# A decoder block on one core: the cross attention's query projection as seven products of halves, its norm factor in the exponential

## The chip, the core and the metric

The kernel runs on one core of a Trainium2 chip. The core has five engines that run beside each other and meet through semaphores: TensorE (PE in the profile, its weight loads PEld), VectorE (DVE), ScalarE (ACT), GpSimd (POOL) and SyncE (SP), which here only starts transfers between the chip's main memory and the core's own SBUF. TensorE writes its sums into PSUM, from which VectorE and ScalarE read them. Each engine works through its own list of instructions in order. The metric is the device time of one execution in microseconds (us).

## The reference, cut to what matters

All is float32, one batch, 512 positions (rows), width 1024, memory of 256 rows. The change lies in the second of three parts of the block:

```
x = x + mixed @ w_out                        # end of the first part
hc    = rms_norm(x, g_cross)                 # x * rsqrt(mean(x*x)+eps) * g, row by row
mem_n = rms_norm(mem, g_mem)
q = (hc @ w_cq)                              # 512x1024 @ 1024x1024, 4 heads of 256
k, v = split(mem_n @ w_ckv)
s = einsum('bshd,bmhd->bhsm', q, k) * 256 ** -0.5
p = softmax(s, axis=-1)
x = x + einsum('bhsm,bmhd->bshd', p, v) @ w_co
hm = rms_norm(x, g_mlp)
x = x + square(relu(hm @ w_up)) @ w_down     # 1024 -> 4096 -> 1024
return rms_norm(x, g_final)
```

## The kernel before

Every float32 factor is split into two halves of lower precision, `hi` and `lo` (`split`: ScalarE rounds the value to `hi`, VectorE subtracts it to get `lo`), and each product is three matmuls, hi by hi, hi by lo and lo by hi, into the same PSUM tile (`mm3`, lines 105 to 107). Activations lie transposed: 128 of the 1024 features on the partitions, positions along the free axis, so a full tile is 128 x 512 and a projection of width 1024 has eight of them. One such tile takes 8 x 3 = 24 matmuls of 512 columns.

**Weights.** All weight blocks, 128 x 1024 each, stand in one list in the order of use. `weights(i)` loads up to four blocks ahead through SP (`wraw`, 3 buffers) and splits up to three ahead (`whi`, `wlo`, 3 buffers each, lines 111 and 112).

**Order.** TensorE runs the program in the order in which it is written. Work of another kind is put between the matmuls by `after(steps, fn)`: a counter goes up by one with every `tick()` (one `mm3` in a projection), and `fn` is emitted when the count is reached; `flush()` emits all that is due. The order on VectorE, ScalarE and the queues is set by a scheduler at build time, from dependences and priorities. Tiles come from pools by tag with a fixed number of buffers; an allocation waits until the oldest tile of its tag has been read for the last time. PSUM has `acc` (2 buffers), `sc` (3), `tr` (2) and `av`.

**The stages around the change, in order:**

- `projection("out", ...)` makes the output projection of the first part, tile by tile. Behind each tile m, `done_out` calls `residual` (line 576: VectorE adds the tile to x, giving `vr`), then `scaled` (ScalarE makes `hi` of x times the gain, VectorE `lo`, line 267) into a pair of tag `xg`, and `accumulate` (ScalarE squares, VectorE adds into `ss`, line 263). `settle()` runs between the first three tiles' parts; it loads x again and puts `mem_in`, the scaling of the memory, into the queue.
- `mem_k(m)`, eight tiles of 128 x 256 in PSUM `acc`, 24 matmuls of 256 columns each. VectorE multiplies each by the memory's norm factor (line 628) and the result is split into `mix`. `stats1`, 16 ticks behind the output projection, sums `ss` over the partitions with two matmuls against ones (lines 236 and 237, behind a split of `ss`) and makes the norm factor `r1` as a full 128 x 512 tile (`rstd_full`). `mem_v`, 96 matmuls of 512 columns, follows.
- The query projection `cq`: eight tiles of 24 matmuls of 512 columns, the first in `sc`, the others in `acc`. VectorE takes each out of PSUM times `r1`/16 (line 734), then it is split into a pair of tag `s`.
- `cross_scores(h)` for head h: 24 matmuls of 256 columns into two `sc` tiles; maximum (line 688), exponential with row sums (line 692), reciprocal and scaling. `cross_transpose(h)`: 8 transposes on TensorE (line 707) into two `tr` tiles, split into an `at` tile. `cross_out(h)`: two `acc` tiles of 6 matmuls of 512 columns each, weights from `mix` (the memory's values), right side from `at`; each tile is split into `xg`. Heads 0, 1 and 2 have their scores, and 0 and 1 their transposes, between the matmuls of `cq`. Behind it stand `cross_out(0)`, scores 3, transposes 2, `cross_out(1)`, `cross_out(2)`; transposes 3 and `cross_out(3)` come 2 and 7 ticks into the next projection.
- `projection("co", ...)`, then `done_co`: residual, and `right_factors(m, t)`, which makes for the MLP's up projection the seven right factors named B11, T1, T2, T3, T4, B21, B22 from halves of the feature axis and of the positions. `up_set` then makes each 512 x 512 block of the up projection from seven products instead of eight (`block_product`, 24 matmuls of 256 columns, twice per product); four left factors are sums of weight quarters (s1 to s4), s1 and s3 made by a second load that GpSimd's queue adds on (`accum_op`), s2 and s4 by VectorE (`combined`).
- `renew()`, between parts of `co`, closes the pool `early` and opens `late` in its space.

Of the kernel before, what the change touches and what calls it, by code (L numbers as in the profile page):

```python
# [50 lines left out]
def block_kernel(ctx: ExitStack, tc: tile.TileContext, x0g, xT, memT, wv, wm, wst, wdn, wckv, wpool, vecs, csts, idn, gfin, out):  # L51
# [5 lines left out]
    late = {}  # L57
# [17 lines left out]

    def sb(tag, shape, bufs, dt=F32):
        p = apool if tag in EARLY_TAGS else late["pool"] if tag in LATE_TAGS else pool
        return p.tile(shape, dt, tag=tag, name=nm(tag), bufs=bufs)
# [73 lines left out]
    def part(n, name):  # L152
        return wst[4 * n + PARTS.index(name)]

    def load(i):
        if i >= len(blocks):
            return
        if isinstance(blocks[i], tuple):
            n, name = blocks[i]
            if name in ("s1", "s3"):  # L160
                first, then = ("A22", "A21") if name == "s1" else ("A21", "A11")
                if (n, name) not in raw:
                    r = fetch((n, name), part(n, first), "mraw", 5)
                    nc.gpsimd.dma_start(r, part(n, then), accum_op=ALU.add)  # L164
            elif name in PARTS:
                fetch((n, name), part(n, name), "mraw" if name == "A11" else "wraw", 5 if name == "A11" else 3)
# [8 lines left out]
    def combined(n, name):  # L175

        if name in ("s2", "s4"):
            r = raw[n, "s1"]
            V.tensor_tensor(r, r, raw[n, "A11" if name == "s2" else "A12"], op=ALU.add)
            return r  # L180
        return raw[n, name]

    def prep(i):
# [3 lines left out]
        r = combined(*blocks[i]) if isinstance(blocks[i], tuple) else raw[i]  # L187
        if i in SPARE:
            hi, lo = (sb("mix", [P, 2, T], 8, F32R).rearrange("p a t -> p (a t)") for _ in range(2))
        elif i >= FIRST_UP and i % 5 > 2:  # L190
# [16 lines left out]
    def weights(i):  # L207
        far = 4 if i >= FIRST_UP else 0
        for j in range(i, i + 4 + far):
            if j < FIRST_UP or late:  # L210
                load(j)
        for j in range(i, i + 3 + far // 2):
            if j < FIRST_UP or late:
# [87 lines left out]
    WU, WQ, WK, WGATE, WOUT, WCQ, WCO = 0, 4, 8, 12, 20, 28, 36  # L301
# [15 lines left out]
    for m in range(KC):  # L317
        where["cq", m] = add(wm[WCQ + m])
# [3 lines left out]
    for g in range(NG):  # L322
        for n in (2 * g, 2 * g + 1):
            for name in FIRST_ORDER if n == 0 else ORDER:
                where[n, name] = add((n, name))
# [248 lines left out]
    def residual(m, o, g=None, ss=None, nxt=None, tag=None):  # L574
        t = res[m]
        V.tensor_tensor(t, o, t, op=ALU.add)
        if ss is None:
            return
        pr = pair(tag, 8)
        scaled(pr[:, 0, :], pr[:, 1, :], t, vec[:, g + m:g + m + 1])  # L580
        accumulate(ss, m, t)
        nxt[m] = (pr[:, 0, :], pr[:, 1, :])
# [69 lines left out]

    ss1 = sb("ss", [P, T], 1)
    x1g = {}

    def done_out(m, o):
        residual(m, o, G_CROSS, ss1, x1g, "xg")

    def settle():
        flush()  # L660
        for m in range(KC):
# [7 lines left out]
    def stats1():  # L669
        st["r1"] = rstd_full(sp1, ss1)  # L670
# [6 lines left out]
    def cross_scores(h):  # L677
        es = []
        for j in range(NT // 2):
            o = ps("sc", 3)  # L680
# [49 lines left out]
    for m in range(KC):  # L730
# [4 lines left out]
        pr = pair("s", 6)  # L735
        split(pr[:, 0, :], pr[:, 1, :], t)
        st["cq", m] = (pr[:, 0, :], pr[:, 1, :])
        if m in (1, 3, 5):
            after(5, cross_scores, m // 2)
        if m in (3, 5):  # L740
            after(2, cross_transpose, m // 2 - 1)
# [10 lines left out]
    right = {n: {} for n in ("B11", "T1", "B21", "B22", "T2", "T3", "T4")}  # L752
    xs, half, rest = {}, {}, []
    A, B = slice(0, M), slice(M, T)

    def parts(name, k, hi, lo, c):
        right[name][k] = (hi[:, c], lo[:, c])

    def right_factors(m, t):

        k = m % 4
        g = vec[:, G_MLP + m:G_MLP + m + 1]
        x = tmp()
        pr = pair("mix", 8)
        if m < 4:
            b12 = tmp()[:, :M]
            S.activation(x[:, A], t[:, A], AF.Copy, scale=g)
            S.activation(b12, t[:, B], AF.Copy, scale=g)
            V.tensor_tensor(x[:, B], x[:, A], b12, op=ALU.subtract)
            xs[k] = (x[:, B], b12)  # L770
            split(pr[:, 0, :], pr[:, 1, :], x)
            parts("B11", k, pr[:, 0, :], pr[:, 1, :], A)
            parts("T1", k, pr[:, 0, :], pr[:, 1, :], B)
            return
        S.activation(x, t, AF.Copy, scale=g)
        t1, b12 = xs[k]
        y = tmp()
# [270 lines left out]
```

## Time and profile before

| | |
|---|---|
| median of 3 runs | 720.37 us (720.23 to 720.95) |
| profiled execution | 720.76 us |
| its span | 719.0 us |
| mean granted clock of TensorE | 0.996 |
| busy: PE, PEld | 707.0 us (98%), 614.4 us |
| busy: DVE, ACT, POOL | 484.7, 409.2, 66.9 us |

The profile shows one execution. The span runs from the first to the last record; the execution's own time is 1.76 us longer. A row of the timeline gives start, duration, engine, source line, operation, output tile <- input tiles and the shape; in brackets stands how long the engine stood idle before it and what ended that. Matmuls overlap in a pipeline, so a matmul's own duration (0.39 us) is longer than the step from one start to the next, and a pace is read from the starts. Numbers behind tile names are left out of the trace.

### The profile page before, as it was taken

Reading aid. Unit: us, or ns where it says so; the run is one execution under the profiler, and the core shown is the slowest. Engines: PE = TensorE matmul, PEld = TensorE weight load, DVE = VectorE, ACT = ScalarE, POOL = GpSimd, SP = SyncE. Lnnn points to the kernel's source line nnn. Section 1 sums busy time; section 2 is a strip of 40 time slices with the busy share of each in tenths; the row PEclk is TensorE's granted clock in tenths of the full one; section 3 lists DMA queues with packets and bytes.
Section 4 is the critical chain, followed back from the end, with each engine's and each line's share of the span. In section 5 each row is a group of like instructions: output and inputs, shape, how many; then the busy total and the mean of one; then the engine's idle time right before and its main releaser. Section 6 shows DMA issues by size and latency. Waiting matters only on the chain.

```text
span 719.0 us, 10284 instructions
## 1 busy us (share of the span) xinstructions
PE 707.0 (98%) x3958; PEld 614.4 (85%) x3958; DVE 484.7 (67%) x761; ACT 409.2 (57%) x691; POOL 66.9 (9%) x59
## 2 busy tenths in 40 slices
PE   9999999999999999999999999999999999999995
PEld 6887887788889888888889988899889998899884
DVE  7597999976888645573886953688337864478633
ACT  7498998677766434352668742377215752257522
POOL 0044111545000000000100000000000000000000
PEclk9999999999999999999999999999999999999998
DMA  8433223143525552213934642268215672043211
GB/s 317 150 118 117 87 76 117 60 131 134 176 89 175 177 167 70 86 58 114 268 88 119 211 141 88 57 180 250 105 54 176 147 234 88 30 118 118 89 59 58
DMA packets 27521, 91.62 MB, mean 127 GB/s; under 512 B 3120, under 2 KB 3248, under 8 KB 27472
## 3 DMA queue, kind: packets, MB, share of 16 engines
q1 hardware_dynamic: 24976, 82.18, 33.7%
q0 software_dynamic: 2352, 8.52, 6.8%
q8 instruction: 31, 0.51, 0.3%
q10 hardware_dynamic: 144, 0.26, 0.1%
q14 instruction: 18, 0.15, 0.1%
HBM read 86.76 MB, written 2.10 MB: 124 GB/s over the span
## 4 chain that ended last, share of the span: by engine, by line
PE 89%; ACT 5%; DVE 4%; issue 1%; POOL 0%; DVEq 0%; ACTq 0%
PE acc L105 14%; PE acc L107 13%; PE acc L106 13%; PE sc L105 10%; PE sc L107 10%; PE sc L106 10%; PE tr L105 4%; PE tr L107 4%; PE tr L106 4%; PE sc L389 1%; ACT tmp L451 1%; PE sc L391 1%; PE sc L393 1%; ACT whi L111 1%; DVE tmp L449 1%
## 5 line engine op out<-in xcount | busy, mean ns | idle before, releaser
L111 ACT CAST whi<-wraw 128x1024 fp32r<-128x1024 f32 (+1 forms) x92 | 95.2, 1035 | 126.5 <-PE tr L107 50.6
L112 DVE TENSOR_TENSOR wlo<-wraw,whi 128x1024 fp32r<-128x1024 f32 (+1 forms) x92 | 112.9, 1228 | 46.4 <-ACT whi L111 45.7
L105 PE MATMUL acc<-xg,whi 128*128 128x512 f32 x256 | 102.1, 399 | 0.0
L107 PE MATMUL acc<-xg,wlo 128*128 128x512 f32 x256 | 100.0, 391 | 0.0
L106 PE MATMUL acc<-xg,whi 128*128 128x512 f32 x256 | 99.7, 390 | 0.0
L107 PEld LDWEIGHTS acc<-xg,wlo 128*128 128x128 f32 x256 | 48.0, 188 | 10.5
L105 PEld LDWEIGHTS acc<-xg,whi 128*128 128x128 f32 x256 | 48.1, 188 | 9.2
L106 PEld LDWEIGHTS acc<-xg,whi 128*128 128x128 f32 x256 | 48.2, 188 | 9.0
L105 PE MATMUL sc<-mix,whi 128*128 128x256 f32 (+1 forms) x184 | 54.9, 298 | 0.0
L164 POOL DMA_DIRECT2D mraw<-wst x16 | 13.9, 866 | 436.7 <-DMA mraw<-wst 357.9
L107 PE MATMUL sc<-mix,wlo 128*128 128x256 f32 (+1 forms) x184 | 54.1, 294 | 0.0
L106 PE MATMUL sc<-mix,whi 128*128 128x256 f32 (+1 forms) x184 | 54.0, 293 | 0.0
L840 DVE SCALAR_TENSOR_TENSOR vr<-acc,sums,vr 128x512 f32<-128x512 f32 x16 | 12.0, 751 | 49.5 <-PE acc L107 49.5
L894 DVE TENSOR_TENSOR tmp<-sc,tmp 128x512 f32<-128x512 f32 x56 | 37.8, 686 | 9.0 <-PE sc L107 8.6
L111 ACT CAST mhl<-wraw 128x1024 fp32r<-128x1024 f32 x18 | 18.9, 1051 | 38.2 <-PE tr L106 27.4
L111 ACT CAST whi<-mraw 128x1024 fp32r<-128x1024 f32 x24 | 25.0, 1050 | 23.3 <-PE tr L107 8.9
L112 DVE TENSOR_TENSOR wlo<-mraw,whi 128x1024 fp32r<-128x1024 f32 x24 | 29.1, 1221 | 10.1 <-ACT whi L111 10.1
L107 PEld LDWEIGHTS sc<-mix,wlo 128*128 128x128 f32 x184 | 34.6, 188 | 1.1
L105 PEld LDWEIGHTS sc<-mix,whi 128*128 128x128 f32 x184 | 34.6, 188 | 1.0
L106 PEld LDWEIGHTS sc<-mix,whi 128*128 128x128 f32 x184 | 34.5, 187 | 1.1
L105 PE MATMUL sc<-s,whi 128*128 128x256 f32 x112 | 31.4, 281 | 0.0
L106 PE MATMUL sc<-s,whi 128*128 128x256 f32 x112 | 31.2, 279 | 0.0
(300 smaller groups left out, 1974.5 us busy)
## 6 DMA issues: line engine op xcount, KB each, us to landing
wraw<-wm SPq DMA_DIRECT2D x44, 512.0 KB, 3.3
wraw<-wdn SPq DMA_DIRECT2D x32, 512.0 KB, 5.1
mraw<-wst SPq DMA_DIRECT2D x24, 512.0 KB, 4.4
wraw<-wckv SPq DMA_DIRECT2D x16, 512.0 KB, 3.2
mraw<-wst POOLq DMA_DIRECT2D x16, 512.0 KB, 7.2
wraw<-wst SPq DMA_DIRECT2D x16, 512.0 KB, 3.4
s<-s SPq DMA_DIRECT2D x8, 256.0 KB, 3.7
vr<-xT SPq DMA_DIRECT2D x8, 256.0 KB, 5.3
```

The source lines that it names most:

```text
L105: nc.tensor.matmul(o, lh, rh, start=start, stop=False)
L106: nc.tensor.matmul(o, lh, rl, start=False, stop=False)
L107: nc.tensor.matmul(o, ll, rh, start=False, stop=stop)
L111: S.copy(hi, src)
L112: eng.tensor_tensor(lo, src, f(hi), op=ALU.subtract)
L164: nc.gpsimd.dma_start(r, part(n, then), accum_op=ALU.add)
L389: nc.tensor.matmul(o[i], xg[k][0][:, tb], wh[:, c], start=k == 0, stop=False)
L391: nc.tensor.matmul(o[i], xg[k][1][:, tb], wh[:, c], start=False, stop=False)
L393: nc.tensor.matmul(o[i], xg[k][0][:, tb], wl[:, c], start=False, stop=k == KC - 1)
L449: V.tensor_tensor_reduce(e[:, :n], o[:, :n], mask[:, T - n:], -0.125, 3.0e38, ALU.add, ALU.min, mn)
L840: V.scalar_tensor_tensor(y, o, sums[:, 2 * NT + t:2 * NT + t + 1], y, op0=ALU.mult, op1=ALU.add)
L894: V.tensor_tensor(u[new], o, u[old], op=ALU.add)
```

## The change

**The query projection.** `cq` becomes two sets, n = 0 and 1, of four of the eight tiles each. A set is made from seven products of halves (`seven`, cut out of `up_set` with the same order and the same sums): each `block_product` is 2 x 4 `mm3` of 256 columns. The seven results are combined on VectorE by seven additions (`plus`) into four quarters C11, C12, C21, C22, and each is split into `s` pairs (`quads`). The right factors are made in `done_out` by the class `Right` (made out of `right_factors`; the MLP uses it too): `add(m)` for m < 4 makes B11 and T1; for m >= 4 it makes B21, B22, T2, T3, and through `finish` T4. These now go to `xg` and `mfac` pairs. The weights of `cq` come as quarters (`wcq`): s1 and s3 by an added second load on GpSimd's queue, s2 and s4 by an addition on VectorE, as for the up projection.

**The norm's factor.** `stats1` makes it per position on the partitions (`rstd_rows`) instead of as a full tile. The scores are made from the unnormed query; in `cross_scores` the factor (/16) multiplies the maximum (a new 128 x 1 VectorE multiplication) and is the `scale` of the exponential.

**Pools and order.** `early` is closed in `settle()`, a new pool `mid` with tags `mfac` (6) and `mraw` (3) stands in its place until `renew()`. Transposed probabilities go to `mfac` pairs. Scores 1 and 0 now go to `acc` tiles, 2 and 7 ticks into the second set, transposes 1 and 0 at ticks 23 and 26. Behind it stand scores 3, `cross_out(1)`, scores 2, `cross_out(0)`, transposes 3, `cross_out(3)`; transposes 2 and `cross_out(2)` come 2 and 7 ticks into `co`. `co` takes its last inputs in another order.

```diff
+    class Right(dict):
...
+        def add(self, m):
+
+            k, t, g = m % 4, res[m], self.gain(m)
+            x = tmp()
+            pr = pair(*self.pair)
+            if m < 4:
+                S.activation(x, t, AF.Copy, scale=g)
+                V.tensor_tensor(x[:, B], x[:, A], x[:, B], op=ALU.subtract)
+                self.kept[k] = x[:, B]
+                split(pr[:, 0, :], pr[:, 1, :], x)
...
+                return
+            S.activation(x, t, AF.Copy, scale=g)
+            b12 = tmp()[:, :M]
+            S.activation(b12, res[k][:, B], AF.Copy, scale=self.gain(k))
+            y = tmp()
+            V.scalar_tensor_tensor(y[:, A], x[:, B], -1.0, self.kept[k], op0=ALU.mult, op1=ALU.subtract)
+            V.tensor_tensor(y[:, B], x[:, B], b12, op=ALU.subtract)
+            p2 = pair(*self.pair2)
+            split(p2[:, 0, :], p2[:, 1, :], y)
...
+        def finish(self, k, x, y, pr):
+            split(pr[:, 0, :], pr[:, 1, :], x)
+            V.scalar_tensor_tensor(y[:, A], y[:, A], -1.0, x[:, A], op0=ALU.mult, op1=ALU.subtract)
...
+            split(self.half[:, 0, c], self.half[:, 1, c], y[:, A])
...
+    rcross = Right(G_CROSS, "xg", 8, "mfac", 6)
 
     def done_out(m, o):
-        residual(m, o, G_CROSS, ss1, x1g, "xg")
+        residual(m, o)
+        accumulate(ss1, m, res[m])
+        rcross.add(m)
+        if m == KC - 1:
+            rcross.last()
...
     def stats1():
-        st["r1"] = rstd_full(sp1, ss1)
+        r = rstd_rows(sp1, NT)
+        st["r1"] = [r[:, 2 * i:2 * i + 1] for i in range(NT)]
+        V.tensor_scalar(r, r, 1.0 / 16.0, None, op0=ALU.mult)
...
-                c = slice(b * M, (b + 1) * M)
-                S.activation(e[:, c], o[:, c], AF.Exp, bias=mx[:, b:b + 1], accum_out=sm[:, b:b + 1])
+                c, r = slice(b * M, (b + 1) * M), st["r1"][2 * j + b]
+                V.tensor_tensor(mx[:, b:b + 1], mx[:, b:b + 1], r, op=ALU.mult)
+                S.activation(e[:, c], o[:, c], AF.Exp, bias=mx[:, b:b + 1], scale=r, accum_out=sm[:, b:b + 1])
...
-        t = sb("at", [P, NT, T], 2, F32R)
-        pt = (t[:, :MT, :], t[:, MT:, :])
+        pt = pair("mfac", 6), pair("mfac", 6)
...
-    for m in range(KC):
-        o = acc() if m else ps("sc", 3)
-        tile_mm(o, W("cq", m), x1g)
-        t = tmp()
-        V.scalar_tensor_tensor(t, o, 1.0 / 16.0, st["r1"], op0=ALU.mult, op1=ALU.mult)
...
+        seven("cq", n, ORDER, rcross, finish)
+
+    cross_query(0)
+    after(2, cross_scores, 1, "acc", 2)
+    after(7, cross_scores, 0, "acc", 2)
+    after(23, cross_transpose, 1)
+    after(26, cross_transpose, 0)
+    cross_query(1)
     flush()
+    cross_scores(3, "sc", 3)
+    cross_out(1)
+    cross_scores(2, "sc", 3)
     cross_out(0)
-    cross_scores(3)
-    cross_transpose(2)
-    cross_out(1)
-    cross_out(2)
-    after(2, cross_transpose, 3)
-    after(7, cross_out, 3)
+    cross_transpose(3)
+    cross_out(3)
+    after(2, cross_transpose, 2)
+    after(7, cross_out, 2)
```

**Where instructions move.** The first place is VectorE between the residual of the last tile of the output projection (the rows that read `acc_2183` before, `acc_2240` after) and the reading of the first `mem_k` tile out of PSUM (line 628 before, 629 after). Before:

```order
L576 TENSOR_TENSOR vr_1903<-acc_2183,vr_1903 128x512
L112 TENSOR_TENSOR wlo_2229<-wraw_2184,whi_2228 128x1024
L267 SCALAR_TENSOR_TENSOR xg_2215<-vr_1903,vx_67,xg_2215 128x512
L263 TENSOR_TENSOR ss_1822<-ss_1822,tmp_2218 128x512
L112 TENSOR_TENSOR wlo_2265<-wraw_2226,whi_2264 128x1024
L112 TENSOR_TENSOR tmp_2222<-ss_1822,tmp_2221 128x512
L628 TENSOR_TENSOR tmp_2256<-acc_2225,mrstd_2139 128x256
```

After, without the first six of the nineteen rows that begin with `vr_1907<-acc_2240` (they are that residual, three splits of right factors and two steps of the memory's norm):

```order
L116 TENSOR_TENSOR wlo_2299<-wraw_2241,whi_2298 128x1024
L232 SCALAR_TENSOR_TENSOR mrstd_2182<-tmp_2183,mrstd_2182 128x256
L116 TENSOR_TENSOR mfac_2231<-tmp_2228,mfac_2231 128x512
L268 TENSOR_TENSOR ss_1822<-ss_1822,tmp_2272 128x512
...
L116 TENSOR_TENSOR wlo_2335<-wraw_2296,whi_2334 128x1024
L701 SCALAR_TENSOR_TENSOR tmp_2228<-tmp_2228,tmp_2223 128x256
L116 TENSOR_TENSOR xg_2276<-tmp_2275,xg_2276 128x512
L116 TENSOR_TENSOR wlo_2389<-wraw_2332,whi_2388 128x1024
L116 TENSOR_TENSOR tmp_2292<-ss_1822,tmp_2291 128x512
L629 TENSOR_TENSOR tmp_2326<-acc_2295,mrstd_2182 128x256
```

Seven rows from the residual to that reading became nineteen. The sum of squares' split (`tmp_2292<-ss_1822`), on which the next matmuls of `stats1` wait, moved behind them too.

The second place is TensorE at the end of the cross attention: the last transposes there (line 707 before, 776 after) and the `cross_out` of the same head. Before, for head 3, inside the first tile of `co`:

```order
L707 MATMUL tr_3263<-ident_70,tmp_3166 128x128 x4
L707 MATMUL tr_3270<-ident_70,tmp_3188 128x128 x4
L105 MATMUL sc_3255<-xg_3216,whi_3002 128x512
L106 MATMUL sc_3255<-xg_3216,whi_3002 128x512
L107 MATMUL sc_3255<-xg_3216,wlo_3003 128x512
...
L105 MATMUL sc_3295<-xg_3137,whi_3097 128x512
L106 MATMUL sc_3295<-xg_3137,whi_3097 128x512
L107 MATMUL sc_3295<-xg_3137,wlo_3098 128x512
L105 MATMUL acc_3299<-at_3262,mix_2674 128x512
```

After, for head 3, ahead of `co` (`mfac_3506` and `mfac_3507` are the halves of the transposed probabilities):

```order
L776 MATMUL tr_3508<-ident_70,tmp_3386 128x128 x4
L776 MATMUL tr_3515<-ident_70,tmp_3410 128x128 x4
L109 MATMUL acc_3522<-mfac_3506,mix_2753 128x512
L110 MATMUL acc_3522<-mfac_3507,mix_2753 128x512
L111 MATMUL acc_3522<-mfac_3506,mix_2753 128x512
```

Fifteen matmuls of `co` stood between the transposes of head 3 and the first matmul that reads them; now none does. The same stretch of `co` matmuls stands between transposes and `cross_out` of head 2.

More of the change, by code (lines that the diff above doesn't have):

```diff
@@ L74, in block_kernel @@
     LATE_TAGS = ("mraw", "mhl", "sums", "few")
+    MID_TAGS = ("mfac", "mraw")
     def sb(tag, shape, bufs, dt=F32):
+        if tag in MID_TAGS and not late:
+            return mid["pool"].tile(shape, dt, tag=tag, name=nm(tag), bufs=bufs)
         p = apool if tag in EARLY_TAGS else late["pool"] if tag in LATE_TAGS else pool
@@ L150, in fetch, with part @@
         return raw[key]
-    def part(n, name):
-        return wst[4 * n + PARTS.index(name)]
+    def part(key, name):
+        return (wcq if key[0] == "cq" else wst)[4 * key[1] + PARTS.index(name)]
     def load(i):
@@ L316, in block_kernel @@
             where["mv", half, k] = add(wckv[KC + 4 * half + k])
-    for m in range(KC):
-        where["cq", m] = add(wm[WCQ + m])
+    FIRST_CQ = len(blocks)
+    for n in range(2):
+        for name in ORDER:
+            where["cq", n, name] = add(("cq", n, name))
     for m in CO_ORDER:
@@ L729, in block_kernel, with seven, plus @@
     mem_v(1)
-    for m in range(KC):
-        o = acc() if m else ps("sc", 3)
-        tile_mm(o, W("cq", m), x1g)
-        t = tmp()
-        V.scalar_tensor_tensor(t, o, 1.0 / 16.0, st["r1"], op0=ALU.mult, op1=ALU.mult)
[L735 to L741, printed above, removed]
+    def seven(key, n, order, factors, finish):
+        u, five = {}, None
+        def plus(new, o, old):
+            if new not in u:
+                u[new] = tmp()
+            V.tensor_tensor(u[new], o, u[old], op=ALU.add)
+        for name in order:
+            o = ps("sc", 3)
+            block_product(W(key, n, name), factors[RIGHT[name]], o)
+            if name == "A11":
+                u["P1"] = tmp()
+                S.copy(u["P1"], o)
+            elif name == "s2":
+                plus("U2", o, "P1")
+            elif name == "s1":
+                five = o
+            elif name == "s3":
+                plus("U3", o, "U2")
+                plus("C22", five, "U3")
+                u["U4"] = u["U2"]
+                plus("U4", five, "U2")
+                finish("22", u["C22"], -1.0)
+            elif name == "A12":
+                plus("C11", o, "P1")
+                finish("11", u["C11"], 1.0)
+            elif name == "A22":
+                u["C21"] = u["U3"]
+                plus("C21", o, "U3")
+                finish("21", u["C21"], -1.0)
+            elif name == "s4":
+                u["C12"] = u["U4"]
+                plus("C12", o, "U4")
+                finish("12", u["C12"], 1.0)
@@ L753, in block_kernel @@
[L753 to L777, printed above, removed]
-        V.scalar_tensor_tensor(y[:, A], x[:, B], -1.0, t1, op0=ALU.mult, op1=ALU.subtract)
-        V.tensor_tensor(y[:, B], x[:, B], b12, op=ALU.subtract)
-        p2 = pair("s", 6)
-        split(p2[:, 0, :], p2[:, 1, :], y)
-        parts("T2", k, p2[:, 0, :], p2[:, 1, :], A)
-        parts("T3", k, p2[:, 0, :], p2[:, 1, :], B)
-        parts("B21", k, pr[:, 0, :], pr[:, 1, :], A)
-        parts("B22", k, pr[:, 0, :], pr[:, 1, :], B)
-        if m < KC - 1:
-            right_rest(k, x, y, pr)
-        else:
-            rest.append((k, x, y, pr))
@@ L800, in done_co @@
+    right = Right(G_MLP, "mix", 8, "s", 6)
     def done_co(m, o):
@@ L802, in done_co @@
             residual(m, o)
[L803 removed]
+            right.add(m)
         if m == KC - 1:
[L805 to L806 removed]
+            right.last()
     def renew():
         flush()
[L811 removed]
+        middle.close()
         late["pool"] = ctx.enter_context(tc.tile_pool(name="late", bufs=1))
[L814 removed]
+    projection("co", cross_o, [0, 1, 2, 3, 6, 7], [4, 5], done_co, renew, CO_ORDER)
     sums = sb("sums", [P, 24], 1)
@@ L924, in down_part, with finish @@
+    def up_set(n, act, j0):
+        q = quads("xg", 8, act.__setitem__, j0)
+        def finish(c, t, sign):
+            hi, lo = q[c]
+            t = two(t)
+            S.activation(t, t, AF.Relu, scale=sign)
+            S.activation(t, t, AF.Square)
+            split(hi, lo, t)
+        seven("up", n, FIRST_ORDER if n == 0 else ORDER, right, finish)
     def down_part(o, t, act, ks, wt, first, last):
```

180 lines of the change are left out of this document (85 added, 95 removed).

## Prediction

> **What bounds the kernel now.** I read the page first: its engines, then the busy time by stretches of the span, then the timeline of TensorE and VectorE at the places the change touches.
>
> ```profile
> span 719.0 us, 10284 instructions
> PE 707.0 (98%) x3958; PEld 614.4 (85%) x3958; DVE 484.7 (67%) x761; ACT 409.2 (57%) x691; POOL 66.9 (9%) x59
> ```
>
> TensorE is busy for 98% of the span, so it bounds the kernel, and only two things count: what its matmuls take, and every wait that arises in its list. VectorE has a third of its time free on the whole, but that is a mean. The next rows (stretch; its length, then busy time and instructions of PE, PEld, DVE, ACT, POOL; granted clock) are the memory's keys, the whole stretch from the query projection to the next projection, and the end of the kernel.
>
> ```profile
> core 0: us, PE busy (x) PEld busy (x) DVE busy (x) ACT busy (x) POOL busy (x), PEclk, DMA share, GB/s
> 215.00:237.00 22.00, 22.00 (x186) 21.70 (x185) 18.35 (x28) 12.98 (x20) 0.00 (x0) 1.00 0.50 168
> 259.50:326.30 66.80, 66.39 (x349) 56.70 (x348) 40.41 (x70) 28.47 (x62) 0.00 (x0) 1.00 0.24 79
> 711.00:712.00 1.00, 0.23 (x1) 0.00 (x0) 0.73 (x1) 0.00 (x0) 0.00 (x0) 1.00 0.65 250
> 712.00:713.00 1.00, 0.00 (x0) 0.00 (x0) 0.18 (x2) 0.72 (x2) 0.00 (x0) 1.00 0.00 0
> 713.00:714.00 1.00, 0.00 (x0) 0.00 (x0) 0.46 (x3) 0.41 (x2) 0.00 (x0) 0.73 0.00 0
> 714.00:715.00 1.00, 0.00 (x0) 0.00 (x0) 0.92 (x3) 0.72 (x1) 0.00 (x0) 0.50 0.00 0
> ```
>
> In the keys' stage TensorE never waits, though VectorE is already busy for 18.35 of 22 us there: it's close to the next bound exactly where the change adds VectorE work just ahead. In the 66.8 us of the attention it waits 0.41 us in all.
>
> **The matmuls saved.** The paces come from starts 24 or 18 matmuls apart: the first pair is one tile of the query projection, the second 18 matmuls of the keys.
>
> ```profile
> 264.94 0.39 PE L105 MATMUL acc<-xg,whi 128*128 128x512 f32 x1
> 270.38 0.39 PE L105 MATMUL acc<-xg,whi 128*128 128x512 f32 x1
> 234.94 0.28 PE L105 MATMUL acc<-s,whi 128*128 128x256 f32 x1
> 237.06 0.40 PE L105 MATMUL sc<-whi,s 128*128 128x512 f32 x1
> ```
>
> 5.44 us / 24 = 0.2268 us for 512 columns; 2.12 / 18 = 0.1178 us for 256. Before, 8 x 24 = 192 wide ones take 43.5 us. After, 2 sets x 7 products x 24 = 336 narrow ones take 39.6 us. The whole stage, from its first matmul to the first of the next projection, takes 66.9 us:
>
> ```profile
> 259.46 0.40 PE L105 MATMUL sc<-xg,whi 128*128 128x512 f32 x1
> 326.34 0.40 PE L105 MATMUL sc<-xg,whi 128*128 128x512 f32 x1
> ```
>
> The saving is 4.0 us, not the eighth (5.4 us) that the count of products promises: two narrow ones take 0.0088 us more than a wide one. The Trainium skill (TensorE: Matmul & The Clock Gate, Part 2) gives an isolated spacing of N/2.4 + 2.5 ns, 215.8 and 109.2 ns; by it an estimate of the saving is 4.7 us. The trace's spacing is wider at both widths and decides here.
>
> **VectorE ahead of the keys.** This is the largest term. The keys' tiles have two PSUM buffers, so the third tile can't start before VectorE has read the first (line 628). What stands on VectorE from the last output tile to that reading, and when the third tile starts (its first matmul is the last row; above it are three rows of the memory's norm, for the price of narrow ones):
>
> ```profile
> 207.52 0.42 DVE L224 SCALAR_TENSOR_TENSOR tmp<-tmp,ssm 128x256 f32<-128x256 f32 x1
> 207.86 0.15 DVE L224 SCALAR_TENSOR_TENSOR rscr<-rscr,rscr 128x4 f32<-128x4 f32 x1
> 207.97 0.43 DVE L227 SCALAR_TENSOR_TENSOR mrstd<-tmp,mrstd 128x256 f32<-128x256 f32 x1
> ...
> 214.07 0.69 DVE L576 TENSOR_TENSOR vr<-acc,vr 128x512 f32<-128x512 f32 x1 [2.14 <-PE acc L107]
> 214.92 1.23 DVE L112 TENSOR_TENSOR wlo<-wraw,whi 128x1024 fp32r<-128x1024 f32 x1 [0.16 <-ACT whi L111]
> 216.06 0.75 DVE L267 SCALAR_TENSOR_TENSOR xg<-vr,vx,xg 128x512 fp32r<-128x512 f32 x1
> 216.72 0.68 DVE L263 TENSOR_TENSOR ss<-ss,tmp 128x512 f32<-128x512 f32 x1
> 217.86 1.23 DVE L112 TENSOR_TENSOR wlo<-wraw,whi 128x1024 fp32r<-128x1024 f32 x1 [0.45 <-ACT whi L111]
> 219.00 0.69 DVE L112 TENSOR_TENSOR tmp<-ss,tmp 128x512 fp32r<-128x512 f32 x1
> 219.60 0.42 DVE L628 TENSOR_TENSOR tmp<-acc,mrstd 128x256 f32<-128x256 f32 x1
> ```
>
> ```profile
> 219.75 0.48 PE L237 MATMUL tr<-tmp,ones 128*128 128x512 f32 x1
> 220.07 0.38 PE L105 MATMUL acc<-s,whi 128*128 128x256 f32 x1
> ```
>
> From start to start, 1024 columns cost 1.14 us (214.92 to 216.06), 512 cost 0.60 (219.00 to 219.60), 256 cost 0.34 (207.52 to 207.86), a tiny one 0.1. Before, the reading ends at 220.02, and the third tile starts at 220.07: it was just in time, as two keys' tiles and the two matmuls of the norm's sum give 5.65 + 0.47 us of cover. After, nineteen instructions stand from the residual through the reading: three of 1024 (3.42), seven of 512 (4.20), eight of 256 (2.72) and a tiny one (0.1), 10.4 us, with the last one's end (0.42 - 0.34) 10.5. The start, 214.07, stays: between the residuals of the last two output tiles VectorE has one of 1024, four of 512, four of 256 and a tiny one, 5.0 us, in the 5.4 us that a tile takes TensorE. So the reading ends at 224.6 and the third tile starts there, not at 220.07: 4.5 us. VectorE also has to wait for ScalarE's rounding in such a row (0.16 and 0.45 us above); I add 0.2 and take **+4.7 us** (bounds 4.5 and 5.5). Below 4.5 it can't go while these instructions stand in this order: an engine works its list off in order, and VectorE had no free time within the row apart from the bracketed waits. From then on VectorE has 1.14 + 0.34 + 0.34 us per tile of 2.83 us and doesn't fall behind again; the norm's smaller form and its tile-wide steps, dropped later, are covered in the same way.
>
> **The clock after that wait.** TensorE then stands for over 4 us with at most one matmul of the norm's sum in it. At the end of the kernel the last matmul ends at 711.23; the granted clock is 1.00 up to 713, 0.73 in the next microsecond, then 0.50: it halves about 2.2 us after the last matmul. What a restart costs shows only at the start of the run.
>
> ```profile
> 1.19 3.60 PE L127 MATMUL acc<-tmp 128*128 128x512 bf16 x8 [1.19 <-DVE tmp L124]
> 4.90 1.62 PE L389 MATMUL sc<-whi,xg 128*128 128x512 f32 x3
> 6.32 0.63 PE L389 MATMUL av<-whi,xg 128*128 128x512 f32 x1
> 6.75 0.93 PE L391 MATMUL sc<-whi,xg 128*128 128x512 f32 x3
> ```
>
> Eight wide matmuls take 3.60 us, 0.45 each, twice the 0.2268 of later; full pace comes between 6.3 and 6.8, about 5.3 us after the first. Half of that time is lost: 2.7 us at most. At least it costs nothing (the wait is too short after all). I take **+2.2 us**, nearer to the upper row. The Trainium skill (the same page, Part 1) puts the drop after a whole idle window of about 3.4 us and the return after as long a busy one; by it the loss would be 1.7 us (an estimate), and a wait of 4.7 us needn't hold a whole window. The trace's drop 2.2 us after the last matmul is sooner than such a window allows, if its start is counted from there.
>
> **The query stage itself.** VectorE's busy 40.4 us get six more weight splits (14 for 8, 6.8 us), four sums of weights (4.6), 14 additions in place of eight readings (3.6) and 16 tiny multiplications (1.6): 57 us of about 64. It's close, but order and prices let it keep step; I take 0 (bounds 0 and the rival below). The waits at the end move:
>
> ```profile
> 323.43 0.50 PE L105 MATMUL acc<-at,mix 128*128 128x512 f32 x1 [0.41 <-DVE xg L112]
> 327.72 1.03 PE L707 MATMUL tr<-ident,tmp 128*128 128x128 f32 x8
> 328.51 0.47 PE L105 MATMUL sc<-xg,whi 128*128 128x512 f32 x1
> 328.42 1.08 ACT L111 CAST at<-tr 128x512 fp32r<-128x512 f32 x2 [1.29 <-PE tr L707]
> 329.03 1.29 DVE L112 TENSOR_TENSOR at<-tr,at 128x512 fp32r<-128x512 f32 x2 [1.19 <-ACT at L111]
> ```
>
> Before, the split of head 3's transposes ends at 329.03 + 1.29 = 330.32, 1.6 us after they do (327.72 + 1.03); fifteen matmuls of the next projection covered that. After, `cross_out(3)` follows at once and its second matmul needs the lower half: **+1.6 us** (1.3 to 2.2, as the splits of `cross_out(0)`, 0.6 us each, may stand ahead). The 0.41 us wait goes, as scores 2 now stand between: **-0.4**. Transposes 2 keep their fifteen matmuls of cover.
>
> **Later stages.** For m < 4 ScalarE makes one 512-wide scaling in place of two of 256, for m >= 4 one of 256 more; in `co` each tile gives them 5.5 us, so nothing. `up_set` issues the same instructions. 0.
>
> **Sum**, against the profiled execution's own 720.76 us (span 719.0 and 1.76 around it): -4.0 + 4.7 + 2.2 + 1.6 - 0.4 = +4.1, so 724.9. That execution is 0.39 above the median; on the median's scale, **724.5 us**.
>
> **The rivals.**
>
> - *No drop of the clock* (0.22): the wait stays, but the one matmul in it or the few microseconds keep the clock. Then +1.9, 722.3. Speaks for it: only one drop is in the trace, at an end where nothing follows.
> - *The second load of the weights comes late* (0.16). s1 of the second set must be loaded, added to by GpSimd's queue, split, and used before the scores that free the `acc` tiles.
>
> ```profile
> mraw<-wst SPq DMA_DIRECT2D x24, 512.0 KB, 4.4
> mraw<-wst POOLq DMA_DIRECT2D x16, 512.0 KB, 7.2
> ```
>
> The first load can only go when a `mraw` buffer comes free (three here, five for the up projection): VectorE's split of the first set's s3, asked for with the third of the set's products of 24 x 0.1178 = 2.83 us, at 5.7, and done by the prices above at some 8.7 us into the stage. With 4.4 and 7.2 us it lands at 20.3; its split is asked for with the eighth product, at 7 x 2.83 = 19.8. Behind that split on ScalarE and VectorE stands the softmax of head 1, which frees the `acc` tiles for the scores of head 0, due at 27.6. That work takes about 5 us, so from a landing at 22.5 on TensorE waits, microsecond for microsecond. An added load half as long again (3.6 us more) gives +1.4, one twice as long +5: 725.9 to 729.5.
> - *The keys' wait doesn't arise, or is made up* (0.09): VectorE needn't be late if the row of nineteen takes 6.0 us, to 220.07, in place of 10.5. Then -4.0 + 1.6 - 0.4 = -2.8, 717.6, faster. Against it: the prices are measured in the same stage, and nothing later could pay back, since all TensorE waits after it in the attention sum to 0.41 us.
> - *The narrow matmuls save nothing* (0.03): the change keeps its word only if 256 columns cost under 0.13 us in the query too (43.5 / 336). The keys, with the same shapes, show 0.1178. Without the saving it is 728.5.
>
> **How the numbers follow.** The forecast case (0.50) is 724.5, with its bounds (clock +0.5 or, of a drop, -1.0; keys +0.8 or -0.2; `cross_out` +0.6 or -0.3) 723.0 to 726.4. No drop gives 721.8 to 723.7, the late load up to 729.5. The range 721.0 to 728.5 leaves out the faster case and the ends of the late load. A difference under 0.2%, 1.4 us, can't be told from none in this kernel: 718.9 to 721.8 holds a third of the no-drop case, if the saving comes out larger, and part of the faster case, 0.11 in all; faster is 0.08; slower, the rest, 0.81.
>
> **What would show it.** In the profile after: a wait of 4 us or more at the first matmul of the third keys' tile or at the second matmul of the norm's sum, put down to VectorE; a granted clock of 0.5 in a slice soon after, and keys' matmuls 0.24 us apart there; query matmuls 0.1178 apart and from the first of them to the first of `co` 64 us instead of 66.9 (-4.0 + 1.6 - 0.4); a wait of 1.3 to 2.2 us at the second matmul of `cross_out(3)`. It is wrong if the third keys' tile starts within 2 us of the second's end, or if TensorE waits over 1 us anywhere within the two query sets; a clock of 1.00 throughout would strike the 2.2.

## The result and the profile after

The changed kernel takes 731.6 us (median of 4 runs, 730.69 to 732.54), the kernel before 720.3 in the same session: 1.0155 times as long, 95% interval 1.0137 to 1.0173. It is slower, as forecast, but by 11.3 us and not by 4.1, and lies outside the range. The profiled execution took 730.69 us with a span of 728.9, so the trace accounts for 9.9 us against the 719.0 of before.

The page of the changed kernel, engines and the chain that ended last:

```profile
span 728.9 us, 10708 instructions
PE 707.5 (97%) x4108; PEld 621.1 (85%) x4108; DVE 507.4 (70%) x818; ACT 425.0 (58%) x719; POOL 70.4 (10%) x63
...
PE 82%; DVE 8%; ACT 6%; DMA 2%; issue 1%; POOL 0%; SPq 0%; DVEq 0%; ACTq 0%
```

TensorE's busy time has hardly moved, the span has grown, and the chain now runs through transfers (DMA 2%), which it didn't before. The trace is cut at three starts on TensorE. The first key matmul (line 105 before, 109 after) starts at 213.87 before and here, as the next rows show, at 216.50; the first query matmul and the first of `co` follow (before: 259.46 and 326.34):

```profile
216.50 0.28 PE L109 MATMUL acc<-s,whi 128*128 128x256 f32 x1
...
271.12 0.28 PE L109 MATMUL sc<-xg,whi 128*128 128x256 f32 x1
...
336.24 0.39 PE L109 MATMUL sc<-xg,whi 128*128 128x512 f32 x1
```

Up to the keys +2.6 us; keys and values 54.62 us for 45.59, +9.0; the query stage 65.12 for 66.88, -1.8; from `co` to the end 392.66 in both, 0. The sum is +9.9; all the loss lies ahead of the query stage.

TensorE's waits, grouped (line, what ended them, total, times, longest):

```profile
PE tr L257 <- DVE tmp L116: 3.4, 1, 3.4
PE tr L256 <- ACT tmp L115: 2.4, 1, 2.4
...
PE tr L241 <- ACT tmp L115: 1.1, 1, 1.1
PE acc L109 <- DVE vr L583: 1.0, 1, 1.0
PE acc L109 <- ACT mfac L115: 1.0, 1, 1.0
...
PE acc L110 <- DVE mfac L116: 0.7, 1, 0.7
```

The first pair is the wait that was forecast, at the sum of squares; the last pair that at `cross_out(3)`. The two in the middle, at the memory's norm (line 241) and at the fourth output tile's buffer (line 583), were not forecast. Both come from late memory input, as the gate below shows, with which both are gone. The transfers that SP issued (start, time that issuing them took):

```profile
177.33 1.28 SPq L153 DMA_DIRECT2D mraw<-wcq  x3
183.31 2.46 SPq L153 DMA_DIRECT2D wraw<-wm  x2
185.82 0.92 SPq L608 DMA_DIRECT2D tmp<-memT  x1
...
189.09 1.01 SPq L608 DMA_DIRECT2D tmp<-memT  x2
```

Three loads of the query's weight quarters, needed at 271, start at 177, with two added loads behind them on GpSimd's queue: `mid` is opened in `settle()`, its buffers are free, and the scheduler lets them go. The next rows give issues, KB of each and the median time to landing between 170 and 215 us, first before, then after:

```profile
tmp<-memT SPq DMA_DIRECT2D x4, 256.0 KB, 3.9
```

```profile
mraw<-wcq SPq DMA_DIRECT2D x3, 512.0 KB, 4.5
mraw<-wcq POOLq DMA_DIRECT2D x2, 512.0 KB, 10.0
tmp<-memT SPq DMA_DIRECT2D x4, 256.0 KB, 8.2
```

The memory's pieces land after 8.2 us in place of 3.9 (the first after 9.6). The three plain loads aren't what lies beside them: the last of the three starts at 178.2 and lands 5.2 us later, at 183.4, before SP issues the memory's first piece at 185.82. The two added loads are still under way: GpSimd issues them from 182.8 on, and they take 8.7 and 11.3 us to land. From 186 to 195 us GpSimd's queue (`software_dynamic`) and the other transfers took (packets, MB, time of the packets as a share of the 16 DMA engines):

```profile
q0 software_dynamic: 285, 1.04, 58.6%
q1 hardware_dynamic: 482, 1.50, 45.1%
```

Together that is all the time that the engines had. In the same stretch before, one queue moved 2.01 MB in 68.3%. ScalarE waits for the first piece of the memory, and VectorE behind it:

```profile
195.46 0.51 ACT L271 ACTIVATE s<-tmp,vx 128x256 fp32r<-128x256 f32 x1 [7.06 <-DMA tmp<-memT]
```

```profile
196.00 0.48 DVE L272 SCALAR_TENSOR_TENSOR s<-tmp,vx,s 128x256 fp32r<-128x256 f32 x1 [5.78 <-ACT s L271]
...
218.27 0.68 DVE L583 TENSOR_TENSOR vr<-acc,vr 128x512 f32<-128x512 f32 x1
...
227.71 0.68 DVE L116 TENSOR_TENSOR tmp<-ss,tmp 128x512 fp32r<-128x512 f32 x1
228.31 0.75 DVE L629 TENSOR_TENSOR tmp<-acc,mrstd 128x256 f32<-128x256 f32 x2
```

ScalarE stood 7.06 us with its list queued behind that scaling, VectorE 5.78 us. The residual of the last output tile starts at 218.27 and not 214.07. From there to the start of the reading of the first key tile it's 10.04 us: the row of nineteen took what the prediction gave it (10.4 less the last one's 0.34). Behind it the norm's small matmuls and the third key tile:

```profile
224.75 0.27 PE L256 MATMUL tr<-ones,tmp 128*128 128x2 f32 x1 [2.44 <-ACT tmp L115]
228.44 0.37 PE L257 MATMUL tr<-ones,tmp 128*128 128x2 f32 x1 [3.42 <-DVE tmp L116]
...
229.96 0.56 PE L109 MATMUL acc<-s,whi 128*128 128x256 f32 x1
230.75 0.41 PE L109 MATMUL acc<-s,whi 128*128 128x256 f32 x1
231.39 0.41 PE L109 MATMUL acc<-s,whi 128*128 128x256 f32 x1
```

Three key matmuls take 0.64 us there, 0.213 each, not 0.1178. Stretches of five microseconds show the clock (the column ahead of the last two):

```profile
225.00:230.00 5.00, 1.58 (x9) 1.56 (x8) 5.00 (x10) 1.67 (x5) 0.00 (x0) 0.69 0.54 176
230.00:235.00 5.00, 5.00 (x29) 5.00 (x30) 2.46 (x10) 1.22 (x5) 0.00 (x0) 0.62 0.08 34
```

### The profile page after: what moved, and what is told of

Same layout as the page of the kernel before. It is cut to its first block, busy times and chain, and to the rows that moved or that the text cites. A ratio compares the mean times of both kernels' runs of the same rounds, so it can differ in the third digit from the quotient of the medians.

```text
span 728.9 us, 10708 instructions
## 1 busy us (share of the span) xinstructions
PE 707.5 (97%) x4108; PEld 621.1 (85%) x4108; DVE 507.4 (70%) x818; ACT 425.0 (58%) x719; POOL 70.4 (10%) x63
## 4 chain that ended last, share of the span: by engine, by line
PE 82%; DVE 8%; ACT 6%; DMA 2%; issue 1%; POOL 0%; SPq 0%; DVEq 0%; ACTq 0%
PE sc L109 11%; PE sc L111 11%; PE sc L110 11%; PE acc L109 10%; PE acc L110 10%; PE acc L111 10%; PE tr L109 4%; PE tr L111 4%; PE tr L110 4%; DMA tmp<-memT 2%; DVE wlo L116 2%; ACT tmp L458 1%; PE sc L396 1%; PE sc L398 1%; PE sc L400 1%
## 5 line engine op out<-in xcount | busy, mean ns | idle before, releaser
L115 ACT CAST whi<-wraw 128x1024 fp32r<-128x1024 f32 (+1 forms) x88 | 90.9, 1034 | 103.1 <-PE tr L111 50.5
L116 DVE TENSOR_TENSOR wlo<-wraw,whi 128x1024 fp32r<-128x1024 f32 (+1 forms) x88 | 107.9, 1228 | 43.1 <-ACT whi L115 42.8
L109 PE MATMUL acc<-xg,whi 128*128 128x512 f32 x200 | 80.1, 401 | 0.0
L111 PE MATMUL acc<-xg,wlo 128*128 128x512 f32 x200 | 78.2, 391 | 0.0
L110 PE MATMUL acc<-xg,whi 128*128 128x512 f32 x200 | 77.9, 390 | 0.0
L115 ACT CAST whi<-mraw 128x1024 fp32r<-128x1024 f32 x34 | 35.5, 1050 | 34.5 <-PE sc L110 10.3
L806 DVE TENSOR_TENSOR tmp<-sc,tmp 128x512 f32<-128x512 f32 x70 | 47.2, 686 | 11.9 <-PE sc L111 11.4
L116 DVE TENSOR_TENSOR wlo<-mraw,whi 128x1024 fp32r<-128x1024 f32 x34 | 41.3, 1222 | 12.7 <-ACT whi L115 12.4
L169 POOL DMA_DIRECT2D mraw<-wst x16 | 13.8, 865 | 332.9 <-DMA mraw<-wst 225.5
L111 PEld LDWEIGHTS acc<-xg,wlo 128*128 128x128 f32 x200 | 37.5, 188 | 8.2
L109 PEld LDWEIGHTS acc<-xg,whi 128*128 128x128 f32 x200 | 37.6, 188 | 7.2
L110 PEld LDWEIGHTS acc<-xg,whi 128*128 128x128 f32 x200 | 37.7, 188 | 7.0
```

The costliest lines, as they stand in the source:

```text
L109: nc.tensor.matmul(o, lh, rh, start=start, stop=False)
L110: nc.tensor.matmul(o, lh, rl, start=False, stop=False)
L111: nc.tensor.matmul(o, ll, rh, start=False, stop=stop)
L115: S.copy(hi, src)
L116: eng.tensor_tensor(lo, src, f(hi), op=ALU.subtract)
L169: nc.gpsimd.dma_start(r, part(key, then), accum_op=ALU.add)
```

## The experiments

Theory A: three separate losses hide a real saving: weight loads sent too early slow the memory input; VectorE's new work stands ahead of the reading of the first key tile, and the clock falls in the wait; the product of head 3 stands right behind its transposes. The rivals: VectorE is overloaded whatever the order (B, F); put-off work comes back (C); the matmuls behind the wait are slow for another reason (D). Each ratio below is to the kernel before, with its 95% interval.

**Holding back the early loads, first try.** The copy into the buffers waits for the memory's last piece:

```diff
             raw[key] = sb(tag, [P, D], bufs)
+            if key[0:1] == ("cq",) if isinstance(key, tuple) else False:
+                V.tensor_copy(raw[key][:, :1], f(st["mg"][KC - 1][0])[:, :1])
             nc.sync.dma_start(raw[key], src)
```

> The changed kernel, but the first loads of the query's weight quarters (three, and what the GpSimd queue adds to two of them) wait for the last piece of the memory input, by a one-column copy into their buffer. Theory A: these loads, issued at 177 us ahead of the memory input, slow it (its first piece took 9.6 us to land against some 3.9 before), ScalarE waits for it with everything queued behind, and VectorE comes 4.2 us late to the last output tile. Then the memory's pieces land in about 4 us again, the last residual starts near 214, and the kernel takes 4 us less than the change: 727.4 (726.5 to 728.5). Theory B: the memory is late because the kept temporary tiles of the new right factors hold up its buffers, or VectorE is simply overloaded there; then the gate changes nothing: 731 to 732.

730.09 us, ratio 1.0138 (1.0123 to 1.0153): between the theories. The memory's pieces landed in 3.8 us and the first query matmul came 3.54 us earlier than in the change (267.58 for 271.12), but the query stage took 2.0 us longer, with a wait of 1.5 us in two pieces:

```profile
PE acc L109 <- ACT tmp L764: 1.5, 2, 1.1
```

The copy had gone into every quarter of both sets. For the second set it stands in VectorE's list in the middle of the query stage and holds the loads back: the second set's first added load lands 23.2 us into the stage, and 20.4 us in the change. The run doesn't decide.

**Holding back the first set's loads alone.**

```diff
             raw[key] = sb(tag, [P, D], bufs)
+            if tag == "mraw" and key[:2] == ("cq", 0):
+                V.tensor_copy(raw[key][:, :1], f(st["mg"][KC - 1][0])[:, :1])
             nc.sync.dma_start(raw[key], src)
```

> The changed kernel with the gate of the first experiment on the first set's three loads alone (that experiment had put the copy into the buffers of the second set too, where it waits in VectorE's list and delays their loads; the scores of head 0 then waited 1.5 us). Theory A, mended: the memory's pieces land in about 4 us as there, the query stage waits no longer than in the change (65.1 us from its first matmul to that of the next projection), and the 3.5 us gained up to the query stage reach the end: 728.1 (727.3 to 729). Theory F: the query stage is bound by VectorE whatever the gate does, and gives 2 us back: 729.5 to 730.5.

727.46 us, ratio 1.0106 (1.0092 to 1.0121), 4.1 below the change (3.2 between the two profiled executions). The memory's pieces land in 4.3 us, and neither of the two unforecast waits is left. The residual:

```profile
214.09 0.68 DVE L585 TENSOR_TENSOR vr<-acc,vr 128x512 f32<-128x512 f32 x1
...
224.47 0.74 DVE L631 TENSOR_TENSOR tmp<-acc,mrstd 128x256 f32<-128x256 f32 x2
```

The residual is back at 214.09, and the reading starts 10.38 us later, behind one instruction more (the row has twenty here). The query stage took 65.11 us, as in the change. Theory A holds for the memory; F falls, and so does B, by which the gate changes nothing. The gate holds back the three plain loads and the two added ones together; that it's the added ones rests on the times in the trace above, as no run delays them alone. Keys and values still take 54.25 us: the wait and the slow clock are there without the late memory.

**Putting off the right factors of tiles 4 to 7.**

```diff
+LATER = {4: 72, 5: 70, 6: 68, 7: 68}
...
-        rcross.add(m)
+        if m < 4:
+            rcross.add(m)
+        else:
+            after(LATER[m], rcross.add, m)
         if m == KC - 1:
-            rcross.last()
+            after(LATER[m], rcross.last)
```

> The changed kernel, but the right factors of output tiles 4 to 7 are made 68 to 72 ticks behind their tile, at the end of the memory's keys and the start of its values, instead of at once. Theory A: the nineteen VectorE instructions ahead of the reading of the first key tile shrink to six, the third key tile hardly waits (under 1 us) and the clock stays up: 4.5 (the row) + 1.2 (the norm's eight small matmuls behind the wait) + 1.8 (half clock) less, 724.1 (723 to 726); the late memory input stays. Theory C: what is put off comes back, because VectorE falls behind in the values' stage and the query products wait for their right factors: less than 3 us gained, 728.5 or more.

725.29 us, ratio 1.0066 (1.0051 to 1.0082), 6.3 below the change and within A's bounds. Keys and values take 46.02 us (54.62 in the change), the wait at the sum of squares is 0.2 us, and the clock stays at 1.00 through both. The row is six instructions:

```profile
218.06 0.69 DVE L584 TENSOR_TENSOR vr<-acc,vr 128x512 f32<-128x512 f32 x1 [1.78 <-PE acc L112]
218.91 1.22 DVE L117 TENSOR_TENSOR wlo<-wraw,whi 128x1024 fp32r<-128x1024 f32 x1 [0.16 <-ACT whi L116]
220.06 0.69 DVE L269 TENSOR_TENSOR ss<-ss,tmp 128x512 f32<-128x512 f32 x1
221.75 1.23 DVE L117 TENSOR_TENSOR wlo<-wraw,whi 128x1024 fp32r<-128x1024 f32 x1 [1.01 <-ACT whi L116]
222.89 0.68 DVE L117 TENSOR_TENSOR tmp<-ss,tmp 128x512 fp32r<-128x512 f32 x1
223.50 0.75 DVE L630 TENSOR_TENSOR tmp<-acc,mrstd 128x256 f32<-128x256 f32 x2
```

TensorE has no wait in the two query sets: C falls. The profiled execution gained 8.6 us in keys and values, though late memory made it start the keys 1.4 us later than the change's, and lost 1.6 again at `cross_out(3)`: the granted clock was 0.76 from 325 to 330 us and 0.90 in the next five, as the next experiment shows in detail.

**Filling the wait.** 56 small matmuls on constants, into a tile that nobody reads, ahead of the norm's sum:

```diff
     def stats1():
+        o = ps("av", 1)
+        for j in range(FILL):
+            nc.tensor.matmul(o[:, :P], ones, ones, start=j == 0, stop=j == FILL - 1)
```

> The changed kernel with 56 matmuls of 128 columns on constants put in TensorE's list just ahead of the norm's sum, into a PSUM tile that nobody reads: they lie in the wait of 6 us and change nothing else. Theory A: the wait stays as long, but the clock doesn't fall; the norm's small matmuls and the first key matmuls behind it run at full pace, 2.4 us less: 729.2 (728.5 to 730). Theory D: the slow matmuls behind the wait are slow for another reason (operands just written): no gain, 731 to 732.

730.71 us (729.37 to 732.39), ratio 1.0149 (1.0130 to 1.0167): by the time alone undecided. By the trace it isn't: keys and values take 52.18 us, 2.44 less than in the change, the clock stays at 1.00 from 215 to 235 us, and the key matmuls run at 0.1178. A holds and D falls for the place in question. What was gained went later: 1.3 us in `co`, in a wait for a residual that the change didn't have and whose cause stays open, and at the end of the attention some 3.4 us run at half pace, as this shows:

```profile
327.34 1.04 PE L780 MATMUL tr<-ident,tmp 128*128 128x128 f32 x8
329.33 0.50 PE L110 MATMUL acc<-mfac,mix 128*128 128x512 f32 x1 [0.95 <-ACT mfac L116]
330.53 0.50 PE L111 MATMUL acc<-mfac,mix 128*128 128x512 f32 x1 [0.70 <-DVE mfac L117]
...
332.62 0.63 PE L112 MATMUL acc<-mfac,mix 128*128 128x512 f32 x1
333.04 0.63 PE L110 MATMUL acc<-mfac,mix 128*128 128x512 f32 x1
```

```profile
330.00:335.00 5.00, 4.47 (x13) 3.58 (x14) 1.16 (x2) 1.03 (x2) 0.00 (x0) 0.68 0.00 0
```

The same two waits (0.95 and 0.70 us) as in the change stand ahead of a lower clock in this execution, and steps of 0.42 us replace 0.23. The change's own profiled execution shows 1.00 there, and so do those of both gates. So the clock falls at `cross_out(3)` in some executions and not in others, which would also spread the change's runs over 1.9 us; that last point is inferred, since those runs have no trace.

**Another order at the end of the attention.**

```diff
     cross_scores(2, "sc", 3)
+    cross_transpose(3)
     cross_out(0)
-    cross_transpose(3)
     cross_out(3)
```

> The changed kernel with the transposes of head 3 put ahead of the product of head 0, so that its twelve matmuls stand between these transposes and the product of head 3. Theory A: the two waits behind the transposes (0.96 and 0.70 us) and the gap at their end go, 2.1 us less: 729.5 (728.8 to 730.3). Theory E: the transposes then wait for the softmax of head 3 by as much, and the time stays within 0.7 us of the change.

729.74 us, ratio 1.0139 (1.0122 to 1.0156), 1.9 below the change. The two waits are gone; one of 0.86 us came, at the first matmul of `cross_out(3)`, which now waits for a tile of `cross_out(0)` to be read out of `acc`:

```profile
331.92 0.50 PE L109 MATMUL acc<-mfac,mix 128*128 128x512 f32 x1 [0.86 <-DVE xg L116]
```

By the traces the query stage is 1.0 us shorter than in the change (64.09 for 65.12), half of what A claimed; the rest of the gain lies ahead of the query stage, where this edit changes nothing. A is right about the waits that go, not about the price.

**The norm's factor alone**, in the kernel before, with its products as they were (`stats1` as in the change):

```diff
-        t = tmp()
-        V.scalar_tensor_tensor(t, o, 1.0 / 16.0, st["r1"], op0=ALU.mult, op1=ALU.mult)
         pr = pair("s", 6)
-        split(pr[:, 0, :], pr[:, 1, :], t)
+        split(pr[:, 0, :], pr[:, 1, :], o)
...
-                S.activation(e[:, c], o[:, c], AF.Exp, bias=mx[:, b:b + 1], accum_out=sm[:, b:b + 1])
+                V.tensor_tensor(mx[:, b:b + 1], mx[:, b:b + 1], r, op=ALU.mult)
+                S.activation(e[:, c], o[:, c], AF.Exp, bias=mx[:, b:b + 1], scale=r, accum_out=sm[:, b:b + 1])
```

> The kernel before with one part of the change alone: the norm's factor per position, in the scale of the exponential and on the maximum; the query's eight tiles, products and right sides stay as they were, and are split straight out of PSUM. Theory A: this part costs nothing on TensorE but the eight small matmuls in place of two wide ones (+0.4) and frees VectorE of eight readings: 720.2 (719.3 to 720.9). Rival: the factor in the exponential lengthens the softmax and the acc tiles are held longer by their split; the attention waits: 721.5 or more.

722.94 us, ratio 1.0037 (1.0024 to 1.0050): the rival's side. The waits name the split (`s`, line 112), not the softmax:

```profile
PE acc L105 <- DVE s L112: 1.4, 1, 1.4
...
PE acc L105 <- DVE xg L112: 0.7, 1, 0.7
```

Splitting straight out of PSUM holds the `acc` tile for ScalarE and then VectorE. So the same with one reading into a temporary tile ahead of the split:

```diff
+        t = tmp()
+        V.tensor_scalar(t, o, 1.0, None, op0=ALU.mult)
         pr = pair("s", 6)
-        split(pr[:, 0, :], pr[:, 1, :], o)
+        split(pr[:, 0, :], pr[:, 1, :], t)
```

> The kernel before with the norm's factor in the exponential, as in the earlier experiment on that part, but each query tile is first read out of PSUM once by VectorE (times 1.0) and then split, as before. Theory A: the 2.5 us of that experiment came from splitting straight out of PSUM, which holds the acc tile for both halves (a wait of 1.4 us at the first matmul of head 0's product, and 0.7 in place of 0.4 at the next): with one reading this part costs only the small matmuls, 720.8 (720.2 to 721.3). Rival: the factor in the softmax itself makes the attention late: 722 or more again.

720.86 us, ratio 1.0010 (1.0001 to 1.0019): the 2.5 us were the form of my edit. The factor in the exponential is all but free.

**All three losses removed.** The gate on the first set and the put-off factors as above, and both last heads inside `co`, which takes its inputs in another order for that:

```diff
     cross_transpose(3)
-    cross_out(3)
-    after(2, cross_transpose, 2)
-    after(7, cross_out, 2)
+    after(4, cross_transpose, 2)
+    after(5, cross_out, 3)
+    after(9, cross_out, 2)
...
-    projection("co", cross_o, [0, 1, 2, 3, 6, 7], [4, 5], done_co, renew, CO_ORDER)
+    projection("co", cross_o, [2, 3, 0, 1], [6, 7, 4, 5], done_co, renew, CO_ORDER)
```

> The changed kernel with three edits: the gate on the first set's loads; the right factors of output tiles 4 to 7 put off by 68 to 72 ticks; at the end of the attention both last heads' products inside the next projection, each a few matmuls behind its transposes. Theory A (three avoidable losses hide the saving): what is left of the change is the saving of its matmuls, 3.3 us by the pace of 0.1197 that the changed kernel shows, less some 0.4 for the norm's small matmuls, with the old waits of 0.4 gone: 717.0 (716 to 718.5), faster than before. Theory F (VectorE is too full in the query stage for this scheme): waits appear in the two sets, and the time is at or above the kernel before, 720.3 or more.

717.76 us (716.83 to 718.43), ratio 0.9963 (0.9951 to 0.9975): faster than before and 13.8 below the change. These are all of TensorE's waits in groups; none lies between the output projection and `co`:

```profile
PE acc L132 <- DVE tmp L129: 1.2, 1, 1.2
PE sc L455 <- DVE small L459: 1.0, 2, 0.8
PE av L111 <- DVE at L117: 0.7, 2, 0.4
PE acc L923 <- ACT vr L925: 0.4, 1, 0.4
PE tr L477 <- DVE tmp L466: 0.3, 1, 0.3
PE sc L399 <- ACT ss L267: 0.3, 1, 0.3
PE sc L110 <- DVE tmp L812: 0.2, 1, 0.2
```

The rest are the start, the first attention, the rows' transposes and the up projection. F falls here too: VectorE keeps up with the scheme.

**The same without the gate.** Only the two lines of the gate are taken out again.

> The kernel with the put-off right factors and the new end of the attention, but without the gate: the first three loads of the query's weights stay ahead of the memory input. Theory A: the memory's pieces take 8 to 10 us again, TensorE waits for the fourth output tile's buffer and for the memory's norm (1.9 and 1.2 us more than with the gate): 720.1 (719 to 721), some 3 us above the kernel with the gate. Rival: with VectorE relieved, late memory is hidden: within 1 us of the kernel with the gate.

720.99 us, ratio 1.0010 (0.9998 to 1.0021), 3.2 above the kernel with the gate, as A has it: `memT` lands in 8.0 us again (3.9 with the gate), the two waits at the memory's norm and the output tile's buffer are back, and the first key matmul starts at 216.34 for 212.90. This pair differs in the early loads alone, with VectorE relieved in both; the rival, that late memory is hidden then, falls.

## Why the prediction was wrong, point by point

The forecast and the profiled execution differ by 5.8 us (+4.1 and +9.9). Late memory is 3.0 of it (2.6 up to the keys, and the 0.4 by which the gate shortens keys and values), the wait of the keys with its clock 1.8 (8.7 for 6.9), the query stage 1.0 (-1.8 for -2.8).

- **What it left out: the added loads of the first set.** The working followed the weight loads of the second set on SP's and GpSimd's queues, for a rival, and never asked what the first set's loads would be in flight with. "The start, 214.07, stays" is the sentence that failed: it was argued from VectorE's work alone, and ScalarE's wait of 7.06 us for a transfer moved the start to 218.27. The memory's place on SP's list isn't what failed it, as its first piece is issued at 185.82 (186.67 before); it shares the DMA engines with the two added loads. Price: 4.1 us by the gate's times (3.2 by its trace), 3.2 by the last pair.
- **The row of nineteen: right.** Some 10.1 us forecast from start to start (10.4 less 0.34), 10.04 measured. The trace's row has six instructions of 512 and nine of 256, not seven and eight; that is 0.3 us less, and the waits for ScalarE make up for it. What was mis-sized is the cost of the wait on TensorE. Seven of the norm's eight small matmuls stand behind the end of `ss`'s split, at half pace some 1.5 us to the third key tile. The prediction let that tile start as soon as the reading ends and called the norm's smaller form covered, without a price. Wait, small matmuls and clock come to 8.7 us (54.25 us of keys and values with the memory on time, 45.59 before), where +4.7 and +2.2 stood; 0.5 of them stay when the row is short too (46.11).
- **The clock: right**, +2.2 forecast, 2.44 measured by the filler (the small matmuls' share of the half pace, some 0.6, in it). TensorE stood from 222.3 to 228.44 with one small matmul in it, longer than forecast, so the rule of the Trainium skill (TensorE: Matmul & The Clock Gate, Part 1), a fall after a whole idle window of about 3.4 us, would have it fall too; this case doesn't separate the two readings. The 2.2 us that the prediction read at the end of the kernel is no fixed delay: in the eleven profiled executions here the granted clock falls 2.0 to 4.7 us after the last matmul.
- **The saving: right in kind, large by 0.7.** The query's narrow matmuls run at 0.1197 us, not at the keys' 0.1178 (336 x 0.0019 = 0.6), so 3.3 us and not 4.0.
- **`cross_out(3)`: under-sized in its price.** 1.6 forecast; the change shows 1.99 us from the start of the transposes to the next matmul and 1.20 to the one after, where 0.82 (the same transposes in the run with the other order) and 0.23 would stand, 2.1 us. In some executions the clock falls there besides, which the prediction saw for the long wait only.
- **The old wait, the transposes of head 2, later stages: right.** From `co` to the end both kernels take 392.66 us.
- **The rivals.** The late added load of the second set didn't occur in the change: no wait over 0.2 us within the two sets. The landing, forecast at 20.3 us into the stage, came at 20.4. Where I delayed it myself, in the first gate, it came at 23.2, past the 22.5 that the prediction gave as the limit, and cost 1.5 us by the mechanism described. In the last run, without the gate, the same wait is 0.34 us.

## What to carry to other kernels

Follow every new transfer from its start to its landing and ask what it now shares the DMA engines with: a load that is free to start early will, and a small input needed soon pays for it. Where buffers are few, count the other engine's instructions that stand ahead of the reading that frees one; new work with a far-off use belongs behind it, and putting it off cost nothing here. A saving of half a per cent on the bounding engine is only seen once each new wait is gone.

## What the runs showed of the hardware

- Beside two added loads of 512 KB in flight, the landing time of a 256 KB load doubled, 3.9 to 8.2 us. From 186 to 195 us the packets of the added loads took 58.6% of the DMA engines' time for 1.04 MB, those of all other transfers 45.1% for 1.50 MB. The Trainium skill (DMA: Bandwidth & Descriptors, Rules for kernel authors) says of two transfers to disjoint halves of the partitions that they share the same engines and serialize; for these whole-width transfers the trace agrees in kind, as the two shares fill the engines.
- The clock can fall in a gap with waits of only 0.95 and 0.70 us and eight transposes: it did in two of the five profiled executions that have this gap (the filler and the put-off factors), and stayed at 1.00 in three (the change and both gates), so it isn't the length alone. With the filler it's 3.5 us from the start of the transposes at 327.34 to steady matmuls at 330.87, and the slow matmuls begin at 331.8, after work had resumed. The Trainium skill (TensorE: Matmul & The Clock Gate, Part 4) says that a transpose doesn't count as busy in the way that other matmuls do. That would fit these two executions, but no run here has the gap without transposes, so it isn't shown.
- By the granted clock, half pace lasted 6.8 us behind the long wait in each of the four profiled executions in which the clock fell there (the change, both gates, the other order), and 3.4 us in both in which it fell at `cross_out(3)`.
- A narrow matmul's spacing differs by stage: 0.1178 us in the keys, 0.1197 in the query sets, with the same shapes. What sets the difference wasn't tried.
